# FFN token operands by ScalarE and GpSimd, the last two merge features in one pass, x tiles ahead of weights

## The chip, the cores and the metric

The kernel runs on one core of a Trainium2 chip. The time is device microseconds of one execution. In the text PE is TensorE's matmul, PEld its weight load, DVE is VectorE, ACT ScalarE, POOL GpSimd and SP SyncE, whose queue issues the DMAs. Lines (L244) are those of the kernel before; after the change the same code stands some lines further down.

## What is computed

One encoder layer on x, 1024 tokens by 1024 features, float32:

```python
x = x + 0.5 * _swiglu(_rmsnorm(x, n1_g[l]), ffn1_w_in[l], ffn1_w_out[l])
h = _rmsnorm(x, n2_g[l])            # projections, mixers a and b
merged = jax.nn.sigmoid(ga) * (o_a @ w_branch_a[l]) + jax.nn.sigmoid(gb) * (o_b @ w_branch_b[l])
x = x + merged @ w_out[l]
x = x + 0.5 * _swiglu(_rmsnorm(x, n3_g[l]), ffn2_w_in[l], ffn2_w_out[l])
return _rmsnorm(x, nf_g)
```

`_swiglu` splits x @ w_in into gate and up (2816 columns each) and returns (silu(gate) * up) @ w_out.

## The kernel before, in words

Every fp32 operand of a matmul is split in a high part (a CAST on ACT, L82) and a low part (a subtraction, L83), and a product takes three matmuls. Each FFN multiplies x by w_in with a scheme of seven block products in place of eight: a gate and an up tile of the weights, cut in two halves of the contraction each, against token blocks b11, b21, b12, b22 (first or second half of the tokens, first or second half of the features). That needs sums of weight blocks (`ffn_weights`, four operations of 128x512 on POOL per tile, L272) and of token blocks (t1 = b12 - b11, t2 = b22 - t1, t3 = b22 - b12, t4 = b21 - t2).

`pair_operands` makes the token operands. A pair is token tile p of the first half and p + 4 of the second. For each of the four pairs it squares both tiles on ACT (L166), makes the reciprocal roots by 128x2 operations on DVE and a Sqrt on ACT, scales x by row factor and gain in one DVE operation per tile (L244, in place), makes four differences on POOL and DVE (L246 to L249), transposes seven blocks on PE (L254) into PSUM and splits them into the operands, the high part on ACT and the low on DVE. Four pairs together fill all seven operands; pairs 0 and 1 are the first 256 of 512 columns, pairs 2 and 3 the rest. `ffn_in` works tile 0 of the weights in two halves of 256 columns, and so can begin on pairs 0 and 1; all other tiles work on 512.

In the first FFN x comes from DRAM, so nothing can be multiplied before the operands are made: this is the kernel's start. In the second FFN x comes from the merge. `merge` goes over eight features i of 128, makes gated activations gh, gl for one, and adds gh @ w_out to x by `out_rows`: per token tile two banks of 512 columns, three matmuls per feature, and one accumulation on DVE (L226). Features are taken in pairs, 0 to 5; 6 and 7 each by themselves, and feature 7 is left to the caller, which does it pair by pair: `rows((t,))` for both tiles of a pair, then `pair_operands` of it. That is the merge's tail.

Engines work their instructions in order; a scheduler lays the program out by priority, each engine's order being what the program text gives as far as buffers allow. `raw` tiles are five buffers of 128x1024 that weights, gains and temporaries share. The pool `sm` holds the weight sums and the discarded output of the Squares. `first` loads x tiles on SP's queue for the first FFN.

## Time and profile before

| | |
|---|---|
| median of three runs | 2464.24 us (2461.96 to 2465.77) |
| profiled execution, its time | 2469.23 us |
| its span | 2467.4 us |
| granted TensorE clock, mean | 0.973 |

The stages in the span: w_in of the first FFN to about 470 us, its w_out to 730, norm to 765, projections and mixers to 1590, merge to about 1780, second FFN with the final norm to the end. A granted clock of 1.00 is TensorE at 2.4 GHz, 0.50 at 1.2 GHz; a stretch in between saw both.

### The profile page before, as it was taken

What the parts mean: (1) busy time and instruction counts of PE and PEld (TensorE: products, weight loads), DVE (VectorE), ACT (ScalarE), POOL (GpSimd) and SP (SyncE); (2) the same over time, 40 slices, a digit from 0 to 9 for tenths busy, and PEclk for the clock granted to TensorE, in tenths of its full rate; (3) what the DMA queues carried; (4) which work ended last, traced back from release to release, by engine and by line L of the source; (5) the groups of instructions that cost most, each with busy time, mean ns of one, the idle gap of its engine ahead of it and who ended that gap; (6) DMA issues with size and microseconds to landing.
All of it is one profiled execution on the core that took longest, in us unless ns stands there. A gap on an engine that the chain in (4) does not pass through costs nothing. (4 is left out here: it accounts for less than half of the span.)

```text
span 2467.4 us, 30513 instructions
## 1 busy us (share of the span) xinstructions
PE 2287.5 (93%) x10928; PEld 1908.3 (77%) x10928; DVE 1642.4 (67%) x3052; ACT 945.3 (38%) x1845; POOL 571.2 (23%) x482
## 2 busy tenths in 40 slices
PE   3999999999999998878888999998699999999997
PEld 3877777778878986766678988877588888878886
DVE  5655555566565579899997378667756655656556
ACT  5444444410024541344443377632444444430002
POOL 3433333200023000222220043220243333410001
PEclk9999999999999999889999999999799999999999
DMA  3333333353322033344423241462233333353332
GB/s 103 113 103 103 103 111 113 111 220 147 128 101 91 18 111 108 95 108 116 111 67 107 86 154 48 140 219 73 86 103 103 111 120 111 103 202 144 130 131 103
DMA packets 204216, 280.81 MB, mean 114 GB/s; under 512 B 12064, under 2 KB 150304, under 8 KB 203552
## 3 DMA queue, kind: packets, MB, share of 16 engines
q1 hardware_dynamic: 204064, 278.86, 34.3%
q8 instruction: 86, 1.41, 0.2%
q14 instruction: 66, 0.54, 0.1%
HBM read 186.55 MB, written 79.69 MB: 108 GB/s over the span
## 5 line engine op out<-in xcount | busy, mean ns | idle before, releaser
L226 DVE SCALAR_TENSOR_TENSOR x<-S,x 128x512 f32<-128x512 f32 x432 | 292.5, 689 | 206.1 <-PE S L118 205.8
L82 ACT CAST whi<-raw 128x1024 fp32r<-128x1024 f32 (+1 forms) x92 | 87.5, 974 | 448.4 <-PE S L118 370.8
L118 PE MATMUL S<-wlo,goh 128*128 128x512 f32 x640 | 249.5, 390 | 0.0
L118 PE MATMUL S<-whi,gol 128*128 128x512 f32 x640 | 249.5, 390 | 0.0
L118 PE MATMUL S<-whi,goh 128*128 128x512 f32 x640 | 245.9, 394 | 3.3 <-DVE bigB L83 1.5
L83 DVE TENSOR_TENSOR wop<-s,wop 128x512 fp32r<-128x512 f32 x168 | 168.3, 1002 | 118.8 <-ACT wop L82 115.5
L292 PE MATMUL mm<-bigA,wop 128*128 128x512 f32 (+1 forms) x736 | 236.5, 384 | 11.1 <-ACT e L316 11.1
L292 PE MATMUL S<-bigA,wop 128*128 128x512 f32 (+1 forms) x736 | 233.1, 380 | 0.0
L83 DVE TENSOR_TENSOR wop<-raw,wop 128x512 fp32r<-128x512 f32 x126 | 114.7, 922 | 169.1 <-ACT wop L82 169.1
L83 POOL TENSOR_TENSOR wlo<-raw,whi 128x1024 fp32r<-128x1024 f32 (+1 forms) x32 | 68.1, 2128 | 499.4 <-ACT whi L82 494.1
L522 DVE TENSOR_SCALAR_CACHE_REDUCE tkj<-sc,stats 128x384 f16<-128x384 int16 (+5 forms) x192 | 180.6, 941 | 3.5
L118 PE MATMUL mm<-bigA,whi 128*128 128x512 f32 x384 | 158.4, 412 | 15.5 <-DVE pwlo L635 10.0
L292 PEld LDWEIGHTS mm<-bigA,wop 128*128 128x128 f32 x736 | 136.7, 188 | 46.6 <-ACT e L316 20.6
L82 ACT CAST wop<-s 128x512 fp32r<-128x512 f32 x176 | 109.2, 622 | 142.4 <-PE mm L292 45.6
L118 PE MATMUL mm<-bigA,wlo 128*128 128x512 f32 x384 | 157.2, 410 | 1.2 <-POOL wlo L83 1.2
L118 PE MATMUL mm<-bigB,whi 128*128 128x512 f32 x384 | 158.0, 411 | 0.2 <-DVE bigB L83 0.2
L292 PEld LDWEIGHTS S<-bigA,wop 128*128 128x128 f32 x736 | 136.6, 188 | 26.2
L573 POOL TENSOR_SCALAR p<-p,z 128x640 f32<-128x640 f32 (+7 forms) x128 | 91.3, 716 | 275.9 <-DVE z L572 206.2
L323 POOL TENSOR_TENSOR e<-e,e 128x512 f32<-128x512 f32 (+1 forms) x46 | 57.1, 1242 | 419.0 <-ACT e L322 419.0
L118 PEld LDWEIGHTS S<-whi,goh 128*128 128x128 f32 x640 | 120.1, 188 | 35.6 <-DVE x L226 8.2
L292 PE MATMUL mm<-bigB,wop 128*128 128x512 f32 (+1 forms) x368 | 140.1, 381 | 0.0
L292 PE MATMUL S<-bigB,wop 128*128 128x512 f32 (+1 forms) x368 | 139.9, 380 | 0.0
(243 smaller groups left out, 5337.2 us busy)
## 6 DMA issues: line engine op xcount, KB each, us to landing
raw<-in_ffn_w_in_dram SPq DMA_DIRECT2D x88, 512.0 KB, 4.3
g_d<-g SPq DMA_DIRECT2D x80, 512.0 KB, 4.8
raw<-in_ffn_w_out_dram SPq DMA_DIRECT2D x44, 512.0 KB, 7.1
goh<-g_d SPq DMA_DIRECT2D x40, 512.0 KB, 5.8
gol<-g_d SPq DMA_DIRECT2D x40, 512.0 KB, 6.7
raw<-in_w_in_dram SPq DMA_DIRECT2D x28, 512.0 KB, 5.3
x<-in_x_dram SPq DMA_DIRECT2D x16, 512.0 KB, 6.1
x_d<-x SPq DMA_DIRECT2D x16, 512.0 KB, 2.6
```

Of the source, the lines that this page charges most:

```text
L82: self.nc.scalar.copy(hi, src)
L83: (eng or self.nc.vector).tensor_tensor(lo, src, hi.bitcast(F32), ALU.subtract)
L118: nc.tensor.matmul(out, lhsT=a, rhs=b, start=(i == 0), stop=(i == len(steps) - 1))
L226: nc.vector.scalar_tensor_tensor(xs, po, scale, xs, ALU.mult, ALU.add)
L292: nc.tensor.matmul(out, lhsT=l, rhs=r, start=start and j == 0, stop=j == len(steps) - 1, skip_group_check=True)
L323: nc.gpsimd.tensor_tensor(e3, e3, e5, ALU.add)
L522: v.tensor_scalar(bits((b + 1) * P), keys[b], cand[:, i:i + 1], 0.0, ALU.is_ge, ALU.add, accum_out=cnt[:, i:i + 1])
L573: nc.gpsimd.tensor_scalar(p, p, z, 1.0, ALU.mult, ALU.mult)
```

## The change

Four things. `pair_operands` scales x by the row factor with a Copy on ACT, multiplies it by the gain on POOL (128x1024), and makes all four differences on POOL, in place where it can; of the 128x2 operations only the reciprocal stays on DVE (`rstds_pool`). `merge` takes features 6 and 7 as a pair, so that the tail has six matmuls per bank where it had three, and one accumulation per bank for both features. In the first FFN, SP loads two more x tiles directly behind the first weights, ahead of cos and sin; tile 0's weights are split with DVE and stand behind the operands of pairs 0 and 1 in the program; in the second, tile 0's weights are loaded ahead of the tail. The weight sums are made in place and in one tile `s` of two buffers; the pool `sm` is gone. The diff, without most of its context:

```diff
@@ -162,7 +162,7 @@
         for i, xt in enumerate(tiles):
-            junk = self.sm.tile([P, D], BF16, tag="s0", name=self.uid("junk"), bufs=1)
+            junk = self.raw()
@@ -240,15 +240,18 @@
         h = D // 2
-        for x, r in zip((x0, x1), self.rstds([x0, x1])):
-            nc.vector.scalar_tensor_tensor(x, x, r, gb, ALU.mult, ALU.mult)
-        ta, tb = self.raw(), self.raw()
-        nc.gpsimd.tensor_tensor(ta[:, :h], x1[:, :h], x0[:, :h], ALU.subtract)
-        nc.vector.tensor_tensor(ta[:, h:], x1[:, h:], ta[:, :h], ALU.subtract)
-        nc.gpsimd.tensor_tensor(tb[:, :h], x1[:, h:], x1[:, :h], ALU.subtract)
-        nc.vector.tensor_tensor(tb[:, h:], x0[:, h:], ta[:, h:], ALU.subtract)
-        for n, src in (("b11", x0[:, :h]), ("b21", x0[:, h:]), ("b22", x1[:, h:]), ("t2", ta[:, h:]),
-                       ("t1", ta[:, :h]), ("t3", tb[:, :h]), ("t4", tb[:, h:])):
+        tt = self.raw()
+        for x, r in zip((x0, x1), self.rstds_pool([x0, x1], tt)):
+            nc.scalar.activation(x, x, AF.Copy, scale=r)
+            nc.gpsimd.tensor_tensor(x, x, gb, ALU.mult)
+        b11, b21, b12, b22 = x0[:, :h], x0[:, h:], x1[:, :h], x1[:, h:]
+        t3, t2 = tt[:, :h], tt[:, h:]
+        def sub(out, x, y):
+            nc.gpsimd.tensor_tensor(out, x, y, ALU.subtract)
+            return out
+        def turn(n, src):
@@ -256,26 +259,65 @@
-    def ffn_weights(self, w_in, i):
+        turn("b11", b11)
+        turn("b21", b21)
+        turn("b22", b22)
+        turn("t3", sub(t3, b22, b12))
+        t1 = sub(b12, b12, b11)
+        sub(t2, b22, t1)
+        turn("t1", t1)
+        turn("t2", t2)
+        turn("t4", sub(b21, b21, t2))
+    def rstds_pool(self, tiles, junk):
+        nc = self.nc
+        n = len(tiles)
+        ms, r, t = (self.small.tile([P, 2], F32, tag=k, name=self.uid(k))[:, :n] for k in ("ms", "rs", "rt"))
+        for i, xt in enumerate(tiles):
+            nc.scalar.activation(junk, xt, AF.Square, accum_out=ms[:, i:i + 1])
+        v = nc.gpsimd
+        v.tensor_scalar(ms, ms, 1.0 / D, EPS, ALU.mult, ALU.add)
+        nc.scalar.activation(t, ms, AF.Sqrt)
+        nc.vector.reciprocal(r, t)
+        v.tensor_tensor(t, r, r, ALU.mult)
+        v.tensor_tensor(t, t, ms, ALU.mult)
+        v.tensor_scalar(t, t, -0.5, 1.5, ALU.mult, ALU.add)
+        v.tensor_tensor(r, r, t, ALU.mult)
+        return [r[:, i:i + 1] for i in range(n)]
+    def ffn_raw(self, w_in, i):
+        out = self.raw(), self.raw()
+        for r, c in zip(out, (i * P, F + i * P)):
+            self.dma(r.rearrange("p (k c) -> p k c", k=KT), w_in[:, c:c + P].rearrange("(k p) c -> p k c", p=P))
+        return out
+    def ffn_weights(self, raws, s):
...
         h = 512
-        rg, ru = self.raw(), self.raw()
-        for r, c in ((rg, i * P), (ru, F + i * P)):
-            self.dma(r.rearrange("p (k c) -> p k c", k=KT), w_in[:, c:c + P].rearrange("(k p) c -> p k c", p=P))
-        sm = [self.sm.tile([P, h], F32, tag=f"s{j}", name=self.uid(f"s{j}"), bufs=1) for j in range(4)]
+        rg, ru = raws
         a11, a12, a21, a22 = rg[:, :h], rg[:, h:], ru[:, :h], ru[:, h:]
-        for out, x, y, op in ((sm[0], a21, a22, ALU.add), (sm[1], sm[0], a11, ALU.subtract),
-                              (sm[2], a11, a21, ALU.subtract), (sm[3], a12, sm[1], ALU.subtract)):
+        s1, s2 = s[:, :h], s[:, h:]
+        def sub(out, x, y, op=ALU.subtract):
             nc.gpsimd.tensor_tensor(out, x, y, op)
-        for j, src in enumerate((a11, a12, sm[1], sm[0], sm[2], sm[3], a22)):
+        sub(s1, a21, a22, ALU.add)
+        sub(s2, s1, a11)
+        sub(a21, a11, a21)
+        for j, src in enumerate((a11, a12, s2, s1, a21, a12, a22)):
...
             self.split(w[:, 0], w[:, 1], src, self.w_eng)
+            if j == 1:
+                sub(a12, a12, s2)
...
-    def ffn_in(self, w_in, ops, ph, g_d, first):
+    def ffn_in(self, w_in, ops, ph, g_d, first, raws):
@@ -293,16 +335,19 @@
         for i in range(NF):
-            self.w_eng = nc.gpsimd if i == 0 else nc.vector
+            self.w_eng = nc.vector
...
                 next(pairs)
-                ws = list(self.ffn_weights(w_in, i))
+                raws = raws or self.ffn_raw(w_in, i)
+                next(pairs, None)
+                ws = list(self.ffn_weights(raws, self.raw()))
...
             else:
-                ws = self.ffn_weights(w_in, i)
-            gh, gl = (ph.tile([P, SEQ], F32R, tag="t4", name=self.uid("g"), bufs=4) for _ in range(2))
+                ws = self.ffn_weights(self.ffn_raw(w_in, i),
+                                      ph.tile([P, 1024], F32, tag="s", name=self.uid("s"), bufs=2))
+            gh, gl = (ph.tile([P, SEQ], F32R, tag="t4", name=self.uid("g"), bufs=self.t4) for _ in range(2))
@@ -337,12 +382,14 @@
-    def ffn(self, x_d, w_in, w_out, g_d, ex, es_ex, first):
+    def ffn(self, x_d, w_in, w_out, g_d, ex, es_ex, first, raws=None):
...
         ops = ex if first is None else self.operands(ex)
-        kept = self.ffn_in(w_in, ops, ph, g_d, (lambda: iter((None,))) if first is None else lambda: first(ops, ph))
+        self.t4 = 4 if first is None else 6
+        kept = self.ffn_in(w_in, ops, ph, g_d, (lambda: iter((None,))) if first is None else lambda: first(ops, ph),
+                           raws)
@@ -824,7 +871,7 @@
             wh, wl = self.weights_cols(w_b, i * P, (i + 1) * P)
-            gp, nb = (last, 1) if i == KT - 1 else (pool, 3)
+            gp, nb = (last, 2) if i >= KT - 2 else (pool, 3)
@@ -851,8 +898,8 @@
                 prev = None
-            if len(cur) == 2 or i >= KT - 2:
-                prev = (cur, [self.weights((w_out[f * P:(f + 1) * P, :], D)) for f in range(i + 1 - len(cur), i + 1)])
+            if len(cur) == 2:
+                prev = (cur, [self.weights((w_out[f * P:(f + 1) * P, :], D)) for f in (i - 1, i)])
@@ -871,7 +918,6 @@
         pairs = [t for p in range(4) for t in (p, p + 4)]
-        self.sm, es_sm = self.open("sm", bufs=1)
@@ -879,7 +925,7 @@
                 for t in ts:
-                    xs[t] = ph.tile([P, D], F32, tag="t4", name=self.uid("x0"), bufs=4)
+                    xs[t] = ph.tile([P, D], F32, tag="t4", name=self.uid("x0"), bufs=6)
@@ -887,12 +933,14 @@
             yield
+            load(pairs[4:6])
+            for p in range(4):
+                if p == 2:
+                    yield
+                    load(pairs[6:])
+                self.pair_operands(ops, xs[p], xs[p + 4], gb, p)
...
             self.dma(self.sin, io["sin"].rearrange("(t p) j -> p t j", p=P))
-            for p in range(4):
-                if p >= 2:
-                    load((p, p + 4))
-                self.pair_operands(ops, xs[p], xs[p + 4], gb, p)
@@ -901,7 +949,6 @@
         close()
-        es_sm.close()
@@ -966,7 +1013,6 @@
-        self.sm, es_sm = self.open("sm", bufs=1)
@@ -977,13 +1023,14 @@
         self.dma(gb, io["n3_g"].partition_broadcast(P))
+        raws = self.ffn_raw(io["ffn2_w_in"], 0)
...
         es_m1.close()
-        x, rows, close = self.ffn(x2_d, io["ffn2_w_in"], io["ffn2_w_out"], g_d[1], ops2, es_ex, None)
+        x, rows, close = self.ffn(x2_d, io["ffn2_w_in"], io["ffn2_w_out"], g_d[1], ops2, es_ex, None, raws)
@@ -992,7 +1039,6 @@
         close()
-        es_sm.close()
```

How the instructions stand. ACT at the start of the kernel, before (wop are weight parts, raw_118 a weight tile, s its sums, x_6, x_7, x_9, x_10 the first four x tiles, junk the discarded squares):

```order
L82 CAST wop_130<-raw_118 128x512
L82 CAST wop_133<-raw_118 128x512
L82 CAST wop_139<-s_13_122 128x512
L82 CAST wop_136<-s_14_123 128x512
L82 CAST wop_142<-s_15_124 128x512
L166 ACTIVATE junk_156,ms_153<-x_6_108 128x1024
L166 ACTIVATE junk_158,ms_153<-x_7_110 128x1024
L82 CAST wop_145<-s_16_125 128x512
L166 ACTIVATE junk_227,ms_224<-x_9_114 128x1024
```

And of the change (raw_123 and raw_193 are the pairs' temporary tiles, raw_115 the weights):

```order
L278 ACT_TABLE_LOAD
L278 ACTIVATE raw_123,ms_124<-x_6_105 128x1024
L278 ACTIVATE raw_123,ms_124<-x_7_107 128x1024
L281 ACT_TABLE_LOAD
L281 ACTIVATE rt_126<-ms_124 128x2
L245 ACTIVATE x_6_105<-x_6_105,rs_125 128x1024
L245 ACTIVATE x_7_107<-x_7_107,rs_125 128x1024
L278 ACTIVATE raw_193,ms_194<-x_9_111 128x1024
L82 CAST wop_267<-raw_115 128x512
L82 CAST wop_270<-raw_115 128x512
L278 ACTIVATE raw_193,ms_194<-x_10_113 128x1024
```

Five casts of weights stood ahead of the first Square; now Square, Sqrt and the scaling of the first two tiles stand ahead of the first cast.

POOL behind the identity matrix, before:

```order
L83 TENSOR_TENSOR wop_130<-raw_118,wop_130 128x512
L83 TENSOR_TENSOR wop_133<-raw_118,wop_133 128x512
L272 TENSOR_TENSOR s_13_122<-raw_119 128x512
L272 TENSOR_TENSOR s_15_124<-raw_118,raw_119 128x512
L272 TENSOR_TENSOR s_14_123<-s_13_122,raw_118 128x512
L83 TENSOR_TENSOR wop_139<-s_13_122,wop_139 128x512
L272 TENSOR_TENSOR s_16_125<-raw_118,s_14_123 128x512
L83 TENSOR_TENSOR wop_136<-s_14_123,wop_136 128x512
L83 TENSOR_TENSOR wop_142<-s_15_124,wop_142 128x512
L83 TENSOR_TENSOR wop_145<-s_16_125,wop_145 128x512
L246 TENSOR_TENSOR raw_169<-x_7_110,x_6_108 128x512
```

And of the change (L280 to L286 the 128x2 operations, L246 the gain, L251 the differences; raw_109 is the gain):

```order
L280 TENSOR_SCALAR ms_124<-ms_124 128x2
L283 TENSOR_TENSOR rt_126<-rs_125 128x2
L284 TENSOR_TENSOR rt_126<-rt_126,ms_124 128x2
L285 TENSOR_SCALAR rt_126<-rt_126 128x2
L286 TENSOR_TENSOR rs_125<-rs_125,rt_126 128x2
L246 TENSOR_TENSOR x_6_105<-x_6_105,raw_109 128x1024
L246 TENSOR_TENSOR x_7_107<-x_7_107,raw_109 128x1024
L280 TENSOR_SCALAR ms_194<-ms_194 128x2
L251 TENSOR_TENSOR raw_123<-x_7_107 128x512
L283 TENSOR_TENSOR rt_196<-rs_195 128x2
L251 TENSOR_TENSOR x_7_107<-x_7_107,x_6_105 128x512
L284 TENSOR_TENSOR rt_196<-rt_196,ms_194 128x2
```

POOL began with the weights' splits and sums and had two differences per pair. Now the first pair's products and differences come first, the second pair's small operations stand between them, and the splits are gone.

PE around the second pair of the merge's tail, before (S_... from ident are the 28 transposes of a pair, four to a row, the rest are rows of feature 7):

```order
L118 MATMUL S_15415<-whi_15289,gl_15155 128x512
L254 MATMUL S_15443<-ident,x_14290 128x128 x4
L254 MATMUL S_15450<-ident,x_14290 128x128 x4
L254 MATMUL S_15457<-ident,x_14290 128x128 x4
L254 MATMUL S_15464<-ident,raw_15437 128x128 x4
L254 MATMUL S_15471<-ident,raw_15437 128x128 x4
L254 MATMUL S_15478<-ident,raw_15438 128x128 x4
L254 MATMUL S_15485<-ident,raw_15438 128x128 x4
L118 MATMUL S_15492<-whi_15289,gh_15154 128x512
```

And of the change (b_3157 and b_3158 are b11 and b21 of the first two pairs, L334 the second FFN's products):

```order
L118 MATMUL S_15282<-whi_15132,gl_15072 128x512
L257 MATMUL S_15308<-ident,x_14213 128x128 x4
L257 MATMUL S_15315<-ident,x_14213 128x128 x4
L334 MATMUL mm_15601<-b_3157_15144,wop_15577 128x256
L257 MATMUL S_15322<-ident,x_14213 128x128 x4
L334 MATMUL mm_15601<-b_3157_15144,wop_15577 128x256 x11
L334 MATMUL tp_15602<-b_3158_15145,wop_15580 128x256 x9
L257 MATMUL S_15330<-ident,raw_15291 128x128 x4
L334 MATMUL tp_15602<-b_3158_15145,wop_15580 128x256 x2
L257 MATMUL S_15339<-ident,x_14213 128x128 x4
L334 MATMUL tp_15602<-b_3158_15145,wop_15580 128x256
L257 MATMUL S_15346<-ident,raw_15291 128x128 x4
```

Products of the second FFN stand between the second pair's transposes, which before came next to one another.

## Rows read from the trace of the kernel before

**Rows 1.** The page's first part: busy us of each engine, share of the span, instructions.

```profile
PE 2287.5 (93%) x10928; PEld 1908.3 (77%) x10928; DVE 1642.4 (67%) x3052; ACT 945.3 (38%) x1845; POOL 571.2 (23%) x482
```

**Rows 2.** The table by stretch: us, then busy us and number of instructions of PE, PEld, DVE, ACT and POOL, the granted clock, the share of the DMA engines, GB/s.

```profile
0.00:28.60 28.60, 0.00 (x0) 0.00 (x0) 3.88 (x13) 10.77 (x18) 12.95 (x16) 1.00 0.46 133
28.60:42.80 14.20, 9.27 (x39) 7.76 (x40) 13.67 (x21) 6.99 (x13) 5.38 (x4) 1.00 0.24 74
42.80:82.00 39.20, 34.52 (x230) 31.73 (x229) 28.95 (x51) 24.06 (x46) 13.66 (x11) 0.87 0.31 95
...
1710.00:1740.00 30.00, 19.48 (x82) 14.93 (x80) 24.21 (x40) 10.81 (x18) 2.49 (x2) 0.83 0.15 61
...
1830.00:2190.00 360.00, 359.32 (x1585) 297.26 (x1585) 218.24 (x246) 160.57 (x283) 128.71 (x95) 1.00 0.34 111
```

**Rows 3.** What PE waited for from 0 to 80 us: engine, line, the instruction waited for; us in total, times, longest.

```profile
PE S L254 <- DVE x L244: 29.6, 2, 28.7
```

**Rows 4.** The same from 1710 to 1806 us.

```profile
PE S L254 <- DVE x L244: 20.4, 4, 5.9
PE S L254 <- DVE raw L247: 7.3, 4, 2.0
```

**Rows 5.** The timeline of PE in the merge's tail: start, us, line, operation (consecutive ones of a kind are put together, with their number).

```profile
1717.41 0.39 PE L118 MATMUL S<-whi,gh 128*128 128x512 f32 x1
...
1733.76 0.78 PE L118 MATMUL S<-whi,gh 128*128 128x512 f32 x1
...
1735.19 0.63 PE L118 MATMUL S<-whi,gh 128*128 128x512 f32 x1
1735.62 0.57 PE L118 MATMUL S<-wlo,gh 128*128 128x512 f32 x1
...
1737.18 0.39 PE L118 MATMUL S<-wlo,gh 128*128 128x512 f32 x1
1737.41 0.40 PE L118 MATMUL S<-whi,gl 128*128 128x512 f32 x1
...
1750.44 0.78 PE L118 MATMUL S<-whi,gh 128*128 128x512 f32 x1
...
1767.33 0.77 PE L118 MATMUL S<-whi,gh 128*128 128x512 f32 x1
...
1788.62 0.60 PE L254 MATMUL S<-ident,raw 128*128 128x128 f32 x4
...
1804.42 0.28 PE L292 MATMUL mm<-bigA,wop 128*128 128x256 f32 x1
```

**Rows 6.** The timeline of DVE and ACT behind the rows of the second pair.

```profile
1736.46 2.08 DVE L226 SCALAR_TENSOR_TENSOR x<-S,x 128x512 f32<-128x512 f32 x3 [0.34 <-PE S L118]
...
1738.63 1.06 ACT L166 ACTIVATE junk<-x 128x1024 bf16<-128x1024 f32 x1 [0.30 <-DVE x L226]
...
1740.01 0.20 ACT L168 ACTIVATE rt<-ms 128x2 f32<-128x2 f32 x1 [0.23 <-DVE ms L167]
...
1741.24 2.48 DVE L244 SCALAR_TENSOR_TENSOR x<-x,rs,raw 128x1024 f32<-128x1024 f32 x2
...
1743.58 0.58 ACT L82 CAST b<-S 128x512 fp32r<-128x512 f32 x1 [3.36 <-PE S L254]
```

**Rows 7.** Groups of instructions on POOL over the whole span: line, operation, shapes, number; busy us, mean ns of one; idle time before them and what ended it.

```profile
L181 POOL TENSOR_TENSOR xn<-x,gain 128x1024 f32<-128x1024 f32 x8 | 19.1, 2394 | 7.2 <-PE S L195 4.6 <-DVE rs L169 2.0 <-DVE x L226 0.5
...
L248 POOL TENSOR_TENSOR raw<-x 128x512 f32<-128x512 f32 x8 | 10.1, 1268 | 0.0
...
L573 POOL TENSOR_SCALAR p<-p,z 128x256 f32<-128x256 f32 x16 | 7.6, 479 | 12.7 <-DVE z L572 10.2 <-PE mm L118 2.3
...
L573 POOL TENSOR_SCALAR p<-p,z 128x128 f32<-128x128 f32 x16 | 5.9, 373 | 33.7 <-DVE z L572 25.4 <-DVE stats L526 6.3 <-PE S L424 1.9
...
L1026 POOL MEMSET const-float32-0.0<- 128x1 f32 x1 | 0.1, 103 | 0.2 <-issue 0.2
```

**Rows 8.** The same on ACT.

```profile
L82 ACT CAST whi<-raw 128x1024 fp32r<-128x1024 f32 x76 | 77.9, 1049 | 434.3 <-PE S L118 359.0 <-issue 41.2 <-DMA raw<-in_w_in_dram 27.7
...
L166 ACT ACTIVATE junk<-x 128x1024 bf16<-128x1024 f32 x32 | 33.8, 1057 | 39.1 <-DVE x L226 30.0 <-DMA x<-in_x_dram 2.7 <-DVE rs L173 2.1
```

**Rows 9.** The timeline at the kernel's start, ACT and DVE.

```profile
12.43 1.14 ACT L82 CAST wop<-raw 128x512 fp32r<-128x512 f32 x2 [10.42 <-DMA raw<-in_ffn_w_in_dram]
...
20.52 1.06 ACT L166 ACTIVATE junk<-x 128x1024 bf16<-128x1024 f32 x1
...
24.43 1.28 ACT L168 ACT_TABLE_LOAD   x1
...
27.27 2.48 DVE L244 SCALAR_TENSOR_TENSOR x<-x,rs,raw 128x1024 f32<-128x1024 f32 x2
```

**Rows 10.** The timeline of PE at the end of tile 0 of the first FFN: the last pair's transposes, and the first instruction of the last product on 256 columns there.

```profile
68.70 1.04 PE L254 MATMUL S<-ident,raw 128*128 128x128 f32 x8
...
79.14 0.28 PE L292 MATMUL S<-bigA,wop 128*128 128x256 f32 x1
```

**Rows 11.** Where POOL and DVE work side by side: two groups on POOL over the whole span, and one weight split on DVE.

```profile
L272 POOL TENSOR_TENSOR s<-raw 128x512 f32<-128x512 f32 x44 | 73.2, 1663 | 4.6 <-DVE wop L83 2.4 <-DMA raw<-in_ffn_w_in_dram 2.1
...
L272 POOL TENSOR_TENSOR s<-raw,raw 128x512 f32<-128x512 f32 x44 | 57.0, 1296 | 87.3 <-DVE wop L83 87.3
...
69.55 1.62 DVE L83 TENSOR_TENSOR wop<-raw,wop 128x512 fp32r<-128x512 f32 x1 [0.50 <-ACT wop L82]
```

## The prediction

> **What bounds the kernel now.** I read the page's share of busy time first: PE works 93% of the span, VectorE 67%, ScalarE 38%, GpSimd (POOL) 23% [rows 1]. So the change can only save or cost time where PE stands still, and the table by stage says where that is [rows 2]. PE has nothing to do until 28.70 us, works 9.27 of the next 14.2 us and 34.52 of 39.2 us to 82 us. From 1710 to 1740 us, the end of the merge, it works 19.48 of 30 us. From 1830 to 2190 us, the second FFN's loop, it works 359.32 of 360 us, and the first FFN's loop is built alike. The change leaves PE's order alone in both loops, so there I expect nothing. Two places remain: the start of the first FFN (A), and the merge's tail with the start of the second FFN (C).
>
> The waits name the cause: before 80 us PE's transposes wait 29.6 us for VectorE's scaling of the token rows, L244 [rows 3]. In the tail they wait 20.4 us, in four waits, for that instruction, and 7.3 us for the differences behind it [rows 4]. In PE's own order the tail shows as twelve matmuls, a stop for the 28 transposes, twelve matmuls [rows 5]: one pair from 1733.76 to 1750.44, the next to 1767.33, 16.7 and 16.9 us apiece, for some 4 us of matmuls. The time between a pair's last accumulation and the next pair's first matmul is what the change touches, and it is a chain of single instructions on ACT, DVE and POOL [rows 6]: 1738.54 to 1750.44, 11.9 us.
>
> **C, the merge's tail.** One pair after the change, link by link from its last accumulation. Both Squares end 1.24 us behind it, as now (1738.54 to 1739.78, [rows 6]). Then ms on POOL, Sqrt 0.2 with its handover, the reciprocal 0.2, four small POOL operations. POOL has no 128x2 operation in the trace. The nearest rows are a 128x1 MEMSET of 0.10 and TENSOR_SCALARs of 0.373 for 128 columns and 0.479 for 256 [rows 7]; the last two make a straight line that meets two columns at 0.27. I take 0.28, near the row of the same kind, and keep 0.10 and 0.37 as ends. Five are 1.4 (0.5 to 1.9), with Sqrt and reciprocal 1.9. Then ScalarE's scaling of x0. No Copy of that shape with a scale per row is in the trace; the Square of 128x1024 takes 1.057 and the CAST of that shape 1.049 [rows 8]; I take 1.06, and since the two rows enclose hardly anything, 0.6 (a 128x512 cast takes 0.59 in [rows 6]) to 1.3 as ends. x1's scaling hides behind POOL. POOL follows with two 128x1024 products of 2.39, the duration at L181, and four 128x512 subtractions of 1.27 (L248) [rows 7]: 4.8 + 5.1 = 9.9. The transposes of t4 end it with about 0.9. Sum: 1.24 + 1.9 + 1.06 + 9.9 + 0.9 = 15.0 us against 11.9, so 3.1 us more per pair and 12.4 for four. The path is longer because what VectorE does in 2.48 for both tiles takes 4.8 on POOL plus 1.06 on ACT, and four subtractions in one queue replace two pairs on two queues.
>
> The Trainium skill, GPSIMD Engine Reference, section 4.1 "Engine selection", gives elementwise work on tiles to VectorE and puts GpSimd at about twice its time for two inputs. The rows agree: 2.39 against 1.24 for the 128x1024 operation. Nothing above is taken from that page.
>
> Adding features 6 and 7 together does not add matmuls; it moves 48 of them from ahead of the tail into it, so the tail's rows begin 48 x 0.227 = 10.9 us earlier and hold 24 matmuls per pair rather than twelve. Twelve take 3.9 us there because the first six or seven after each stop run at half clock (0.43 apart, then 0.23 [rows 5]); 24 take 6.6. The 16 accumulations (L226, 0.69 each) that go away are VectorE's; around 1710 us it is the bound for about 1 us, which I credit. So the tail starts at 1717.4 - 10.9 - 1 = 1705.5. A pair is then 6.6 + 0.75 (last accumulation) + 15.0 = 22.4 us. The first has weight splits of the added feature ahead on VectorE, 0.5 more. The fourth has three more weight casts on ACT and four splits on DVE ahead of its Sqrt and reciprocal, because the second FFN's weights are now loaded ahead of the pairs, and half-clock FFN matmuls among its transposes: 4.2 more. Together 4 x 22.4 + 0.5 + 4.2 = 94.3, and the last operand is transposed at about 1800 where it now is at 1789.2 (1788.62 + 0.6): 10.8 later. Against that, PE's new order has FFN2 products of the first token half between the second pair's transposes, where before they come only in the fourth's. That leaves 12.7 us of work from the last transpose to the instruction from which both orders agree again (mm<-bigA at 1804.42), where now 15.2 us pass. C = 10.8 - 2.5 = **+8.3 us**. Its ends: with the small operations at 0.10, the scaling at 0.6 and no delay in the fourth pair, +0.6; with 0.37, 1.3 and twice that delay, +15. I count +4 to +14 as its own range.
>
> **A, the start of the first FFN.** Now ACT casts weights first, at 12.43, when they land, and only then squares x at 20.52, so the scaling comes at 27.27 and PE at 28.70 [rows 9]. After the change, x's Squares stand first in ACT's queue. x lands at about 4.2 (its Square's start is not in the trace of before; the weights, issued behind five other loads, are there at 12.43). Two Squares 2.4, ms 0.28, table load and Sqrt 1.5, reciprocal and small ones 1.3, scaling 1.06: POOL's first product starts at 10.7 and PE's first transposes at 13.2, 15.5 us earlier.
>
> But this stage ends with the last pair's operands, now transposed from 68.70 on [rows 10]. POOL now does four pairs of 9.9 and the four weight sums of 1.28: 44.7 us and 4 us of small ones, where it had eight subtractions. Pair 0 is through at 22.2, pair 1 with the sums at 37.3. Then ACT's queue stops it: the third pair's Square needs a raw buffer that frees only when the weights in it are split, at about 34.5; behind it come three more Squares of 1.2, casts of 0.6 for pair 1's operands, and two table loads of 1.28 (Silu, then Sqrt again). The Sqrt comes at 44.5, the product at 47.3. Two pairs of 9.9 and some waiting end at 70.7, the transposes at 71.3. Behind them stand about 10 us of PE work in both orders (68.70 to the row at 79.14 [rows 10]). A = 71.3 - 69.7 = 1.6, plus 0.4 for half-clock matmuls after longer stops: **+2 us**. Ends: -8.5 if POOL runs pairs 2 and 3 straight behind pair 1, +6 if POOL's products are slowed as its adds already are in [rows 11].
>
> **The rest.** The weight splits of tile 0 move from POOL (1.3) to DVE, and cos and sin behind x13 and x14 on SP's queue: both hidden behind POOL's 44.7 us, and the price if uncovered is 7 x 0.69 = 4.8 us, inside A's ends. The weight sums in place and in two buffers instead of one remove a wait of POOL that ends long before PE needs the operand; PE's loop has 0.7 us in 360 to give [rows 2]. Pool `sm`'s removal moves addresses only. The scheduler also reorders part of the mixer stage; I find no term with a sign there and count 0, ends -5 and +5.
>
> **Sum.** +8.3 + 2 = +10.3 us. Against the profiled 2469.2 that is 2479.5; that execution lay 5 us over the median 2464.24, so the median of the changed kernel should be **2474.5 us**. 0.2% (5 us) is what this measurement can tell from no change.
>
> **Rivals.**
> - *The head start stays.* It decides at one point: POOL's first product of pair 2 begins before about 39 us. ACT's queue then was not in the way, A is -8.5, and if the small operations are near 0.10 as well (5 x 0.18 x 4 = 3.6 off C), the sum is 8.3 - 3.6 - 8.5 = -3.8, about 2460; with the mixers' share on the same side, faster. For it: PE's 15.5 us. Against: two table loads and four Squares in one queue. Chance 0.2, 0.12 of it faster by 0.2%.
> - *The tail hides it.* FFN2 products fill the waits of pairs 1 to 3 better than I walked; at C's lower end of +1 the sum is +3, 2467, no change. Against: only two of seven products are ready before pairs 2 and 3. Chance 0.15.
> - *POOL and DVE slow one another.* POOL's adds from raw take 1.66 on average against 1.296 and a weight split on DVE 1.62 against 0.69 when both run [rows 11]. If all POOL work of the pairs takes 1.28 times as long, 2.8 us more per pair and eight pairs make +22, 2497; half of it, 2486. Against: at the tail DVE reads PSUM then, and the 0.69 beside POOL's work stays. The skill's GPSIMD Engine Reference, section 1, says that the two share SBUF interfaces, with contention for VectorE instructions of two SBUF inputs; that agrees with these rows. Chance 0.1.
>
> My forecast holds 0.55. Range: 2459 to 2487, from the first rival to half of the third. Chances: faster 0.16 (0.12, and 0.04 from the mixers), same 0.2, slower 0.64.
>
> **What the profile would show.** Right: PE's first transposes near 13 us, the last operands of tile 0 near 71; in the tail, pair periods of 22 to 27 us with POOL busy nearly 10 us in each and PE waiting for POOL's subtractions in place of L244 and L247; the FFN loops unchanged. Wrong: pair 2's product before 39 us, small POOL operations far from 0.28, the transposes' wait in the tail under 12 us, or several us gone between 765 and 1590 us.

## The result

The changed kernel takes 2481.41 us (median of four runs, 2480.41 to 2483.80) against 2464.26: 1.0072 times as long, interval 1.0054 to 1.0089. It is slower by 0.7%, inside the range, by 17 us where 10 were forecast. The profiled executions differ by 12.1 us only (spans 2479.5 and 2467.4): that of before lay 5 us over its median, that of the change at its own.

The table by stretch of the changed kernel, to lay beside [rows 2]:

```profile
0.00:28.60 28.60, 7.68 (x33) 5.61 (x34) 10.87 (x17) 17.46 (x27) 18.66 (x26) 0.85 0.67 206
28.60:42.80 14.20, 9.36 (x50) 7.60 (x48) 8.74 (x10) 11.06 (x20) 10.82 (x9) 0.74 0.13 38
42.80:82.00 39.20, 24.84 (x143) 22.59 (x144) 13.10 (x22) 18.30 (x31) 28.56 (x27) 0.68 0.19 55
1710.00:1740.00 30.00, 20.28 (x79) 15.31 (x78) 12.71 (x20) 12.85 (x19) 10.69 (x11) 0.72 0.09 36
1740.00:1770.00 30.00, 16.08 (x82) 13.36 (x80) 9.19 (x15) 12.78 (x21) 12.88 (x17) 0.79 0.17 70
1770.00:1800.00 30.00, 16.88 (x82) 13.59 (x83) 12.26 (x19) 13.07 (x22) 22.46 (x20) 0.75 0.27 88
1830.00:2190.00 360.00, 360.00 (x1590) 298.08 (x1589) 204.89 (x248) 160.66 (x284) 132.38 (x93) 1.00 0.36 111
```

PE starts 15 us earlier and has done 7.68 us of work by 28.60 us, where it had done none. But from 42.80 to 82 us it works 24.84 us and not 34.52, at a granted clock of 0.68. In the merge's tail it works 16 to 20 us of each 30. The second FFN's loop is full, as before. What PE waited for there, columns as in [rows 3], from 0 to 84 us (the first three lines) and from 1700 to 1820 us (the last two):

```profile
PE S L257 <- POOL x L246: 21.2, 4, 13.5
PE S L257 <- POOL x L251: 8.3, 6, 3.8
PE S L257 <- POOL raw L251: 7.9, 5, 2.8
...
PE S L257 <- POOL x L246: 33.3, 6, 9.2
PE S L257 <- POOL x L251: 1.8, 4, 0.7
```

L246, the product with the gain on POOL, has taken the place of L244 in [rows 3, 4], with 33.3 us in the tail against 20.4. All waits for the pairs' products and differences there come to 36.5 us, where L244 and L247 had 27.7.

Where the 12.1 us lie is seen from the start of the same instruction on PE in every trace: the transposes of the last pair's last block in the first FFN (head), the first instruction of its w_out (loop 1), from the first transposes of the norm to the first matmul of the merge (norm and mixers), to the last block's transposes in the second FFN (merge and tail), to the last product of w_in there (loop 2). Stretches in us, of the trace of each kernel (the last column is the median of its runs, and a trace is of one of them):

| kernel | head | loop 1 | norm, mixers | merge, tail | loop 2 | median |
|---|---|---|---|---|---|---|
| before | 69.1 | 425.5 | 856.5 | 199.6 | 421.7 | 2464.3 |
| e0, before again | 69.0 | 425.7 | 860.2 | 199.4 | 421.7 | 2464.3 |
| changed | 75.7 | 425.5 | 854.0 | 209.8 | 419.7 | 2481.4 |
| e1 | 66.4 | 409.5 | 857.4 | 194.3 | 435.4 | 2458.8 |
| e2 | 75.8 | 425.6 | 855.7 | 212.2 | 419.8 | 2486.8 |
| e3 | 57.4 | 425.6 | 853.9 | 194.4 | 419.3 | 2447.0 |
| e4 | 81.0 | 409.6 | 855.5 | 228.2 | 421.1 | 2491.2 |
| e5 | 54.8 | 425.7 | 858.9 | 195.8 | 419.2 | 2444.9 |
| e6 | 61.4 | 410.7 | 857.3 | 197.1 | 416.2 | 2437.4 |
| e7 | 67.3 | 410.9 | 851.8 | 193.0 | 422.6 | 2444.4 |
| e8 | 57.4 | 409.1 | 855.0 | 195.9 | 416.2 | 2424.7 |
| e9 | 60.5 | 409.1 | 853.0 | 193.3 | 416.2 | 2429.6 |

Changed against before: head +6.6, loop 1 0.0, norm and mixers -2.5, merge and tail +10.2, loop 2 -2.0.

### The profile page after: what moved, and what is told of

It is laid out like the page before. It is cut to its first block, busy times and chain, and to the rows that moved or that the text cites. A ratio compares the mean times of both kernels' runs of the same rounds, so it can differ in the third digit from the quotient of the medians.

```text
span 2479.5 us, 30627 instructions
## 1 busy us (share of the span) xinstructions
PE 2287.6 (92%) x10928; PEld 1905.1 (77%) x10928; DVE 1577.8 (64%) x2978; ACT 962.0 (39%) x1861; POOL 625.9 (25%) x540
## 3 DMA queue, kind: packets, MB, share of 16 engines
q1 hardware_dynamic: 204064, 278.86, 34.4%
## 5 line engine op out<-in xcount | busy, mean ns | idle before, releaser
L226 DVE SCALAR_TENSOR_TENSOR x<-S,x 128x512 f32<-128x512 f32 x416 | 281.7, 689 | 207.6 <-PE S L118 205.9
L83 DVE TENSOR_TENSOR wop<-raw,wop 128x512 fp32r<-128x512 f32 x224 | 166.0, 750 | 207.9 <-ACT wop L82 207.2
L334 PE MATMUL mm<-bigA,wop 128*128 128x512 f32 (+1 forms) x736 | 237.4, 385 | 10.6 <-ACT e L361 10.6
L334 PE MATMUL S<-bigA,wop 128*128 128x512 f32 (+1 forms) x736 | 233.3, 380 | 0.5 <-DVE bigB L83 0.5
L82 ACT CAST wop<-raw 128x512 fp32r<-128x512 f32 x224 | 137.1, 625 | 100.2 <-PE mm L334 45.3
L334 PEld LDWEIGHTS mm<-bigA,wop 128*128 128x128 f32 x736 | 137.6, 189 | 45.9 <-ACT e L361 19.8
L83 DVE TENSOR_TENSOR wop<-s,wop 128x512 fp32r<-128x512 f32 x84 | 92.3, 1098 | 119.6 <-ACT wop L82 119.3
L334 PEld LDWEIGHTS S<-bigA,wop 128*128 128x128 f32 x736 | 136.6, 188 | 26.9 <-DVE bigB L83 0.7
L83 POOL TENSOR_TENSOR wlo<-raw,whi 128x1024 fp32r<-128x1024 f32 (+1 forms) x32 | 69.4, 2169 | 282.2 <-ACT whi L82 272.6
L334 PE MATMUL mm<-bigB,wop 128*128 128x512 f32 (+1 forms) x368 | 140.4, 382 | 0.0
L334 PE MATMUL S<-bigB,wop 128*128 128x512 f32 (+1 forms) x368 | 139.8, 380 | 0.0
L118 PEld LDWEIGHTS S<-whi,gol 128*128 128x128 f32 x640 | 120.1, 188 | 25.4
```

The source lines that it names most:

```text
L82: self.nc.scalar.copy(hi, src)
L83: (eng or self.nc.vector).tensor_tensor(lo, src, hi.bitcast(F32), ALU.subtract)
L118: nc.tensor.matmul(out, lhsT=a, rhs=b, start=(i == 0), stop=(i == len(steps) - 1))
L226: nc.vector.scalar_tensor_tensor(xs, po, scale, xs, ALU.mult, ALU.add)
L334: nc.tensor.matmul(out, lhsT=l, rhs=r, start=start and j == 0, stop=j == len(steps) - 1, skip_group_check=True)
```

## The experiments

**e0, the kernel before again.**

> The kernel before, unchanged, timed against itself and profiled anew. Expected by all theories: ratio 1.000 within 0.2%, and the same waits as in the first profile (PE's transposes wait 29.6 us before 80 us and 27.7 us in the merge's tail). It settles one thing: the profiled execution of before took 2469.2 us and its unprofiled ones 2464.3, while those of the change agree (2481.3 and 2481.4). If the new profile lies near 2464, the first was 5 us long by chance, and the comparison of the two traces gives 12.1 us where the times give 17.1; if it lies at 2469 again, profiling lengthens the kernel before and not the changed one.

Measured: 0.9999 of before (0.9987 to 1.0010), ten runs from 2460.07 to 2472.32, of which the profiled one is the longest. Its trace has the waits of the first in head and tail, and 3.6 us more in norm and mixers, with the same program. So in norm and mixers differences within some 4 us, and in single executions' times within some 8, say nothing. The profiled execution of this kernel was a long one both times, 5 and 8 us over the median; whether that is chance, two executions do not show. Against the median of before beside e0, 2465.98 of 17 runs, the change costs 15.4 us.

**e1, the pairs' engines as before.** In place of the Copy, the product and four POOL differences (the 128x2 operations go back to DVE too, and a pair has two temporary tiles again; the cut shows two of the lines put in):

```diff
-            nc.scalar.activation(x, x, AF.Copy, scale=r)
-            nc.gpsimd.tensor_tensor(x, x, gb, ALU.mult)
+            nc.vector.scalar_tensor_tensor(x, x, r, gb, ALU.mult, ALU.mult)
...
+        nc.vector.tensor_tensor(ta[:, h:], x1[:, h:], ta[:, :h], ALU.subtract)
```

> The changed kernel with the engines of the pair's operands as before: row factor and gain in one DVE operation per tile, two differences on POOL and two on DVE, the 128x2 operations on DVE. The order of loads, tile 0's weights behind the first two pairs, features 6 and 7 together and the weight sums stay changed. Theory 1 (the chain of ScalarE and GpSimd in the pairs is the loss): the tail's wait behind a pair's last accumulation falls from about 16 to 12 us, four times 4 us; at the start PE's first transposes stay near 13 us and the last of tile 0 come at 55 to 62 us in place of 75.7. Together 2448 to 2460 us, faster than both. Theory 2 (the merge's tail lost because 48 matmuls moved into it, and the start because of the new order of ACT's queue): about 2472 to 2480, little better than the change. Theory 3 (the reordered mixers and the moved buffers): no change from 2481.

Measured: 2458.78 us, 0.9970 of before (0.9959 to 0.9980). Merge and tail fall by 15.5 us, the head by 9.3 (to 66.4, not to 55 to 62): theory 1 holds. The table shows something else that no theory had: against the changed kernel loop 1 is 16.0 us shorter and loop 2 15.7 longer, with the same instructions, so that the total hides it. e4 and e7 take that up.

**e2, features 6 and 7 apart.**

```diff
-            if len(cur) == 2:
+            if len(cur) == 2 or i >= KT - 2:
```

> The changed kernel with features 6 and 7 added apart again, as before: the tail has twelve matmuls per pair, 16 more accumulations on DVE. All else stays changed. Theory 1: nearly neutral, 2478 to 2486: 48 matmuls go back ahead of the tail, the waits per pair stay 16 us, and about 1 us of DVE-bound matmuls comes back. Theory 2: the tail is as long as before the change, 2471 to 2475.

Measured: 2486.84 us, 1.0087 (1.0071 to 1.0104), 5.4 more than the change. Theory 2 falls: the features apart are no faster. 2.5 us of the difference lie in merge and tail; the rest is in norm and mixers, where e0 moved as much by itself.

**e3, the scaling alone back on DVE.** The first three lines of e1's diff; differences and small operations stay on POOL.

> The changed kernel with row factor and gain in one DVE operation per tile again (1.24 us each) in place of a Copy on ACT and a product on POOL; the four differences and the small operations stay on POOL. Theory 1: per pair the chain loses 1.2 + 4.66 and gains 2.48, so 3.4 us less per pair: 13 us in the tail (wait 12.7 per pair), and at the start POOL has 9.3 us less to do per two pairs, so that the last operands of tile 0 come at about 62 to 67 us: 2456 to 2466 us. If the four differences in one queue are the greater part of the loss instead, the wait stays at 14 us or more and the time at 2470 or more. Theory 2: 2474 to 2481.

Measured: 2446.98 us, 0.9923 of before (0.9908 to 0.9938): 34.4 us less than the change, 19 less than before beside it. Head -18.3 and merge and tail -15.4 make up nearly the whole of it. The edit takes back the Copy and the product at once, so the runs do not divide the loss between ScalarE and POOL. One pair of the tail in the timeline of e3:

```profile
1719.97 0.20 POOL L285 TENSOR_TENSOR rs<-rs,rt 128x2 f32<-128x2 f32 x1
1720.20 2.48 DVE L245 SCALAR_TENSOR_TENSOR x<-x,rs,raw 128x1024 f32<-128x1024 f32 x2 [1.14 <-POOL rs L285]
...
1722.76 1.27 POOL L250 TENSOR_TENSOR raw<-x 128x512 f32<-128x512 f32 x1 [2.60 <-DVE x L245]
...
1726.83 1.28 POOL L250 TENSOR_TENSOR x<-x,raw 128x512 f32<-128x512 f32 x1
```

The row factor is ready at 1720.17 (1719.97 + 0.20), both tiles are scaled at 1722.68 and the differences end at 1728.11; in the changed kernel the same takes from 1745.09 to 1756.45, 3.4 us longer, as expected. The head gave more than I expected: 57.4 us in place of 62 to 67. Against e1 the tail is the same (194.4 and 194.3) and the head 9.0 us shorter: differences and small operations on POOL cost nothing in the tail, and the scaling is the loss there. How the 9.0 us divide among them, the order of the transposes and the temporary tiles, in which e1 differs too, is not shown.

**e4, before with the new pairs alone.** `pair_operands` and `rstds_pool` of the change in the kernel before.

> The kernel before with one part of the change alone: the pairs' operands by ScalarE and GpSimd. Theory 1 (the chain of ACT and POOL in the pairs is the loss): PE's wait in the merge's tail rises from 27.7 to 41 to 46 us (about 4 us per pair, +16), and at the start POOL does its 10 us per pair behind the weight splits and sums that it still has there: +8 to +14. Besides, PE's order in the first FFN's loop is another here (the product with b21 stands between those with t2 and t3). If it is this order that decides whether PE waits 0.45 us for ACT's copy in each of its passes (theory of the loop, from the run with the pairs as before, where the first FFN took 16 us less and the second 14 us more), the loop gives back 14 to 16 us: 2474 to 2482 in all. Without the theory of the loop: 2488 to 2496. Theory 2 (the order of loads and the merge are the loss, the pairs are not): 2462 to 2468, or 2448 to 2452 with the loop.

Measured: 2491.24 us, 1.0106 (1.0089 to 1.0124), 9 us above the upper end of what was expected with the loop. That it lies in the range without the loop (2488 to 2496) is chance: loop 1 is 16.0 us shorter, as the order of products said, and merge and tail are 28.6 longer where 16 were expected. With twelve matmuls a pair the tail is free of everything else: rows start at 1751.42 and, a pair later, at 1772.07, so 20.65 us against the 16.9 of [rows 5]. The chain costs 3.8 us per pair; I had worked out 3.1. The miss is in the fourth pair, by the timeline of POOL in e4:

```profile
1780.32 0.20 POOL L286 TENSOR_TENSOR rs<-rs,rt 128x2 f32<-128x2 f32 x1
1783.45 2.52 POOL L83 TENSOR_TENSOR wop<-raw,wop 128x512 fp32r<-128x512 f32 x2 [2.94 <-ACT wop L82]
1785.92 1.27 POOL L302 TENSOR_TENSOR s<-raw 128x512 f32<-128x512 f32 x1
1787.15 1.29 POOL L302 TENSOR_TENSOR s<-raw,raw 128x512 f32<-128x512 f32 x1
1788.39 2.36 POOL L246 TENSOR_TENSOR x<-x,raw 128x1024 f32<-128x1024 f32 x1
...
1791.93 2.38 POOL L246 TENSOR_TENSOR x<-x,raw 128x1024 f32<-128x1024 f32 x1
...
1796.75 2.50 POOL L83 TENSOR_TENSOR wop<-s,wop 128x512 fp32r<-128x512 f32 x2
...
1810.67 1.26 POOL L251 TENSOR_TENSOR x<-x,raw 128x512 f32<-128x512 f32 x1
```

Weight splits and sums of the second FFN's first tile, L83 and L302, stand between that pair's products and differences: from its row factor (1780.52) to its last difference (1811.93) 31 us pass, where 11.3 do in the third pair. The change has those splits on DVE and loads the weights ahead of the tail; there the fourth pair takes 11.7 us for the same (1790.65 to 1802.35).

**e5, a tile of its own for the discarded squares,** on e3:

```diff
-            junk = self.raw()
+            junk = pool.tile([P, D], BF16, tag="junk", name=self.uid("junk"), bufs=1)
```

> The run with the scaling on DVE (2447), and the discarded Squares of the norms in a tile of their own again in place of a raw buffer. In every kernel with the change the norm stage before the projections is 3 to 5 us longer, and PE waits 4.3 us there for the first projection weights' cast. Theory of the buffer: a Square holds one of five raw buffers, so the load of those weights is late; with a tile of its own the wait goes, and the time falls by 3 to 5 us, to 2442 to 2444. If the mixers' stage behind it takes up the 4 us, as it took up part of the change's delay, or the order of the loads is the cause: 2446 to 2448.

Measured: 2444.89 us, 0.9923 (0.9901 to 0.9944), the same ratio as e3. The wait at the end of the norm, 720 to 785 us, stands first among PE's waits in e3:

```profile
PE mm L118 <- ACT whi L82: 4.4, 1, 4.4
```

In e5 it is gone, and the first of PE's waits there is another:

```profile
PE S L195 <- POOL xn L182: 2.1, 1, 2.1
```

So the buffer theory is right about the wait and its price does not reach the end: norm and mixers together are 851.8 to 860.2 us in all traces, with and without it.

**e6, e7, e8: the order of the seven products.** e7 is the kernel before with this edit alone, e6 is e5 with it, e8 is e5 with it from the second weight tile on (the order of the weights in `ffn_weights` goes with it):

```diff
-                product(by, next(w), ops["b21"], cols, True)
-                product(bx, next(w), ops["t2"], cols, False)
-                nc.scalar.copy(e2, bx)
-                nc.vector.tensor_tensor(e1, by, e1, ALU.add)
                 product(bz, next(w), ops["t1"], cols, True)
                 nc.scalar.copy(e5, bz)
+                product(bx, next(w), ops["t2"], cols, False)
+                nc.scalar.copy(e2, bx)
+                product(by, next(w), ops["b21"], cols, True)
+                nc.vector.tensor_tensor(e1, by, e1, ALU.add)
```

> The kernel before with the same order of the seven products and nothing else changed. Theory of the loop: 14 to 16 us less in the first FFN, nothing in the second, where this order stood already: 2448 to 2452. If the loop's time hangs on something else that the change moved (buffers, the weight sums): 2462 to 2466.

> The run before this one with the seven products of the FFN written in the order b11, t1, t2, b21, t3, b22, t4, so that in both FFNs 12 matmuls of another bank stand between the product with t2 and the one with t3 while ACT copies the bank. Theory of the loop: PE's 0.45 us wait for the copy goes in the first FFN too, 0.75 us per tile with the slower first matmul behind it, 21 tiles: 14 to 16 us, 2427 to 2430. If the wait only moves to another copy or to the weights' splits, whose order changes with it: 2440 or more.

> The run with scaling on DVE, own junk tile and the new product order, but the order only from the second weight tile on; tile 0 has its products as in the change. With the order everywhere, tile 0's operands ended at 61.4 us where they ended at 54.8 without, since the product with t1 now comes before that with b21 and PE's queue waits for t1 while pairs are still being made. If that is so, the head comes back to about 55 us and the loop stays without its wait: 5 to 7 us less than 2437, about 2430 to 2433. If the head's loss has another cause, or the scheduler puts the same order into tile 0 anyway: 2436 to 2439.

Measured: e7 2444.39 us, 0.9919 (0.9899 to 0.9938), 20 us less than before, where 14 to 16 were expected: 14.6 lie in loop 1, and merge and tail, where nothing was expected, are 6.6 us shorter; e6 2437.40, 0.9889 (0.9872 to 0.9906), 7 us above the range of its theory and below that of the rival; e8 2424.70, 0.9847 (0.9825 to 0.9869), 5 us below its range and the best version, 40 us under before and 57 under the change. In the first FFN of before, PE ran t2's product and then, one matmul on, t3's into the same bank, so it waited for ACT to copy t2's sum out, as its timeline shows (the product with t2, one matmul of another bank, the first with t3):

```profile
133.38 2.88 PE L292 MATMUL mm<-t,wop 128*128 128x512 f32 x12
136.10 0.39 PE L292 MATMUL S<-bigA,wop 128*128 128x512 f32 x1
136.93 0.50 PE L292 MATMUL mm<-bigA,wop 128*128 128x512 f32 x1 [0.45 <-ACT e L316]
```

In the second the scheduler had put b21's product between them. The program text is the same for both, so it does not settle the order alone. Among PE's waits of before, 100 to 450 us, it is this line:

```profile
PE mm L292 <- ACT e L316: 7.6, 17, 0.5
```

In e1 the scheduler chose the other order in each FFN, and the same wait stands among PE's waits from 1850 to 2150 us:

```profile
PE mm L320 <- ACT e L347: 6.7, 15, 0.5
```

The table by stretch of before for 100 to 450 us, and of e7 for both loops, where PE waits for nothing that is listed:

```profile
100.00:450.00 350.00, 342.37 (x1489) 278.06 (x1488) 206.41 (x232) 148.91 (x266) 129.68 (x90) 1.00 0.33 105
...
100.00:450.00 350.00, 350.00 (x1545) 289.80 (x1545) 216.82 (x243) 158.20 (x280) 142.22 (x94) 1.00 0.36 112
1850.00:2150.00 300.00, 300.00 (x1325) 248.43 (x1324) 182.09 (x206) 134.83 (x238) 119.04 (x79) 1.00 0.36 112
```

Loop 1 gains 14.6 us by it, 0.70 for each of 21 tiles: 0.45 is the listed wait, the rest lies in PE's busy time. In merge and tail, 20 matmuls of the second FFN's first tile stand between the last two blocks' transposes in before, which start 4.0 us apart (1784.62 and 1788.62), and none in e7, where it is 0.85; that is 3.2 of the 6.6 us there, and loop 2 is 0.9 longer. In e6 the head is 6.6 us longer than in e5; in e8 it is 4.0 us shorter than in e6, so tile 0's order was a part of that and the rest stays open. The trace of e8 is of its longest run, 2430.80 us.

**e9, two differences on DVE,** on e8: t2 and t4 by `nc.vector`.

> The run before this one with two of the four differences (t2 and t4) on DVE, as before the change, and t3 and t1 on POOL. The prediction put part of the loss on four differences in one queue. If they are on the path: 1.27 becomes 0.69 twice per pair, 0.5 to 1.2 us less per pair in the tail, 2 to 5 us less in all. If DVE's two-input difference is slowed beside POOL's work (1.73 us for it in the trace of before) or the differences are not on the path: no change, within 1.5 us of the run before this one.

Measured: 2429.56 us, 0.9862 (0.9837 to 0.9887): not faster than e8; the intervals overlap. The tail is 2.6 us shorter and the head 3.1 longer. With the scaling on DVE, the four differences in one queue cost nothing that the time shows; that they are not what the change lost by in the tail rests on this and on e1 beside e3.

## Why the prediction was right in direction and short in size

*What bounds the kernel:* right. The loss lies where PE stands still, the head and the tail; loop 1 kept its time (425.5 in both), and the 2.0 us that loop 2 gave are in C. The prediction took the first FFN's loop to be full because the second's was; it was not (342.37 of 350 us). That is no term of the sum, since the change left PE's order alone there; e7 shows what mending it is worth.

*C, +8.3 us:* merge, tail and loop 2 together came to +8.2. Its terms, by the second pair of the merge in the timeline of the changed kernel (start and length in us, engine, line, operation, tile written and tiles read, and in brackets the wait before it and who ended it):

```profile
1741.34 0.69 DVE L226 SCALAR_TENSOR_TENSOR x<-S,x 128x512 f32<-128x512 f32 x1 [0.67 <-PE S L118]
...
1743.36 0.19 POOL L280 TENSOR_SCALAR ms<-ms 128x2 f32<-128x2 f32 x1 [10.04 <-ACT raw L278]
...
1744.07 0.19 POOL L283 TENSOR_TENSOR rt<-rs 128x2 f32<-128x2 f32 x1 [0.52 <-DVE rs L282]
1744.34 0.20 POOL L284 TENSOR_TENSOR rt<-rt,ms 128x2 f32<-128x2 f32 x1
...
1744.89 0.20 POOL L286 TENSOR_TENSOR rs<-rs,rt 128x2 f32<-128x2 f32 x1
1745.12 2.19 ACT L245 ACTIVATE x<-x,rs 128x1024 f32<-128x1024 f32 x2 [1.34 <-POOL rs L286]
1746.35 4.66 POOL L246 TENSOR_TENSOR x<-x,raw 128x1024 f32<-128x1024 f32 x2 [1.26 <-ACT x L245]
...
1751.09 1.27 POOL L251 TENSOR_TENSOR raw<-x 128x512 f32<-128x512 f32 x1
...
1755.16 1.29 POOL L251 TENSOR_TENSOR x<-x,raw 128x512 f32<-128x512 f32 x1
...
1757.46 0.63 PE L257 MATMUL S<-ident,x 128*128 128x128 f32 x4 [0.26 <-DVE bigB L83]
...
1758.05 0.50 PE L118 MATMUL S<-whi,gh 128*128 128x512 f32 x1
```

Small operations follow each other at 0.28 (1744.07, 1744.34), the value taken; their work is 0.19 of it. The scaling holds POOL back 1.26 us (1.06 taken), the two products take 4.66 (4.8), the four differences 5.36 from the first start to the last end (5.1), and the transposes behind them end another 1.6 later (0.9), since products of the second FFN stand between them on PE; 0.26 of it is a wait for a bank. Last accumulation (1742.03) to the next pair's rows (1758.05): 16.0 us, where 15.0 were worked out; it is 16.2 in the first pair and 14.8 in the third. The fourth took 17.6 from its last accumulation to the end of its last block (1785.79 to 1803.39), where the sum had 19.2. So the size of C is right in the main, and in part by misses that cancel. One sign was misread: PE's wait is for L246, the product, and hardly for the differences (33.3 against 3.2 us in the tail).

*A, +2 us:* it was +6.6; this is the term that was mis-sized. Up to the third pair the walk held: first transposes 13.54 (13.2 forecast), first pair through at 22.46 (22.2), second at 39.28 (37.3), third pair's product at 46.57 (47.3). Then I let two pairs of 9.9, with 3.6 us of waiting, run one behind the other to 70.7, and the last transposes follow within 0.6. They did not, as the timeline of POOL in the changed kernel shows:

```profile
46.57 9.31 POOL L246 TENSOR_TENSOR x<-x,raw 128x1024 f32<-128x1024 f32 x4 [0.55 <-ACT x L245]
55.84 2.49 POOL L251 TENSOR_TENSOR raw<-x 128x512 f32<-128x512 f32 x2
58.29 2.49 POOL L251 TENSOR_TENSOR x<-x,x 128x512 f32<-128x512 f32 x2
60.73 1.27 POOL L308 TENSOR_TENSOR s<-raw 128x512 f32<-128x512 f32 x1
61.95 2.48 POOL L251 TENSOR_TENSOR raw<-x 128x512 f32<-128x512 f32 x2
64.40 1.26 POOL L308 TENSOR_TENSOR s<-s,raw 128x512 f32<-128x512 f32 x1
65.62 1.26 POOL L308 TENSOR_TENSOR raw<-raw,raw 128x512 f32<-128x512 f32 x1
66.84 1.26 POOL L251 TENSOR_TENSOR x<-x,raw 128x512 f32<-128x512 f32 x1
71.12 1.28 POOL L251 TENSOR_TENSOR x<-x,raw 128x512 f32<-128x512 f32 x1 [3.02 <-PE S L257]
```

The timeline of PE there:

```profile
63.27 1.12 PE L257 MATMUL S<-ident,raw 128*128 128x128 f32 x4 [2.54 <-POOL raw L251]
68.16 3.57 PE L257 MATMUL S<-ident,x 128*128 128x128 f32 x16 [3.77 <-POOL x L251]
...
75.74 0.60 PE L257 MATMUL S<-ident,x 128*128 128x128 f32 x4
```

POOL made four products in a row, then the differences of both pairs in turn, with three weight sums of the next tile (L308) between, 3.8 us that the sum had not counted there. So both pairs' operands came at the end together; PE, whose queue holds the pairs in order, stood at the third pair's last block until 68.16, and POOL's last difference, which overwrites b21, waited 3.02 us for PE to transpose it. POOL was through at 72.40, 1.7 us later than forecast; the other 2.7 are PE's, which from 68.16 on worked without a stop through the transposes and first products that had piled up. The last block came at 75.74 and not at 71.3. This is read from the trace; no run put the two pairs one behind the other.

*The rest:* features together were credited with 1 us and gave 2.5 in the tail. "Pool `sm`'s removal moves addresses only" was wrong: the Squares then held raw buffers, and PE waited 4.3 us for a weight load; it cost nothing in the end (e5). The mixers' term of 0, -5 to +5, was -2.5, which e0 does not tell from nothing.

*The rivals:* the head start did not stay, though PE started as early as said. FFN2 products did fill waits, but not more than walked. POOL and DVE slowed each other only in places of the head; in the tail POOL's durations were those of [rows 7].

*The sum:* the traces say +12.1 where the sum had +10.3. That they lie so near is in part luck: A was 4.6 us short, and norm and mixers, without a term, took 2.5 off. The medians say 15.4 to 17.1. The difference between traces and medians lies in executions of the kernel before, whose profiled one was 5 us over its median; where those 5 us come and go is not settled. The Trainium skill's rule on engine selection (GPSIMD Engine Reference, section 4.1) points the same way as e3: with row factor and gain in one operation on VectorE the kernel takes 34 us less.

## What to carry to other kernels

On a chain that one engine waits for, shares by engine are not the measure: count the links and their durations, and where the same queue serves several such chains, look at the order in which it takes them, not at the sum of their work. Here a product that added to a bank which ACT was still copying out waited 0.45 us for it in each of 17 passes; a product with another bank between took the wait away. Before judging a few us by traces, run the same kernel twice and see which stage moves by itself. And read a run by stages even where its total is as expected: in e1 and e4 two differences in other stages cancelled or covered one another.

## What was not expected of the hardware

On POOL a 128x2 operation takes 0.19 us and follows another that it depends on after 0.28; on DVE such operations follow at 0.20 in the trace of before (1740.45 and 1740.65 us). POOL's price lies in the large operands: 2.33 us for 128x1024, where DVE does factor and gain together in 1.24.

A wait of 0.45 us in front of one matmul cost 0.70 us per pass. The matmuls of that bank (mm<-bigA) take 397 ns on average in loop 1 of before and 389 in loop 2, which is some 0.13 us for 16 of them; the remaining 0.12 has no row.
